# Gate products of a recurrence as pairs over 64 rows, with their activations in one table, in a hybrid decoder layer

## The chip, the cores and the metric

The kernel runs on one core of a Trainium2 chip. The metric is the device time of one execution in microseconds (us). Three runs of the kernel before took 961.67, 961.89 and 962.27 us; the median is 961.89 us.

A core has five engines that work at the same time, each on its own list of instructions in a fixed order: TensorE (PE, matrix products), VectorE (DVE), ScalarE (ACT, activation functions), GpSimd (POOL) and SyncE (SP, which here only issues DMAs). A product has two instructions on PE: a weight load (its row in the profile has the engine name PEld) and the matmul that streams the other operand through the array. Engines wait for each other through semaphores.

## The reference

One decoder layer over 1024 tokens and 16 meta tokens, model width 1024, feed-forward width 4096:

```
u = rmsnorm(h) ;  z = u @ w_in = [q | k | v | x_rec | y_rec]
B = sliding-window attention(q, k, v, sinks)                # 8 heads of 64
xr = causal depthwise conv of width 4 over x_rec            # 512 channels
gate_r = einsum("btnc,ncd->btnd", xr in 8 blocks of 64, w_a) + b_a
gate_i = einsum("btnc,ncd->btnd", xr in 8 blocks of 64, w_x) + b_x
r, i  = sigmoid(gate_r), sigmoid(gate_i)
log_a = -8 * r * softplus(-lambda) ;  a = exp(log_a)
u     = sqrt(-expm1(2 * log_a)) * (i * xr)
h_t   = a_t * h_(t-1) + u_t                                 # along the tokens
A = gelu(y_rec) * h
h += rmsnorm(concat(B, A) @ w_out)
h += rmsnorm(w_ff2 @ relu(w_ff1 @ rmsnorm(h))^2)
```

The gates are products with eight separate blocks of 64x64 weights, one for each 64 channels.

## The kernel before

Every product is made in three parts. An operand is split into a high part (fp32r, made by a cast) and a low part (what is left, made by a subtraction), and `mm3` (lines 122 to 128) multiplies high x high, high x low and low x high into one PSUM bank. The helper `split` (lines 93 to 100) makes the two parts: the cast on ACT (line 95) or on another engine (line 97), the subtraction on DVE (line 98).

The kernel runs in stages: norms, k, v and first q; attention over four head pairs, two halves each; gates and recurrence; output projection; the feed-forward part, in which most of the time is spent. The projections of further q, x_rec and y_rec columns are "fills": `next_fill` (lines 658 to 664) loads the weights of the fill after this one and issues the products of this one, and while attention waits for ACT or DVE, PE has these products. A scheduler of the framework sets the order of each engine's instructions from its own estimate of durations and from priorities. `deferred` (lines 73 to 76) lowers the priority of what is in it, `behind` (lines 105 to 113) fixes that one instruction stands after another in the schedule, without a semaphore, and `lut` (lines 81 to 91) keeps the activations that need a function table in the order in which the program writes them, since ACT holds one table at a time and a change of table is an instruction of its own (ACT_TABLE_LOAD).

The recurrence is held transposed: 512 channels as four chunks `c` of 128 channels (two blocks of 64) on the partitions, 1040 tokens along the free axis. Its steps are:

- The weights of the two gates are laid out as 128x128 matrices with two blocks of 64x64 on the diagonal and zeros elsewhere (`graw`, lines 683 to 693): POOL writes the zeros, four DMAs the blocks, and `split` makes `gh` and `gl`.
- `gates(c)` (lines 697 to 715): for each of two gates and each of three pieces of 348, 348 and 344 tokens, one `mm3` with all 128 rows, and one Sigmoid from PSUM, with the bias in it. That is 4 x 2 x 3 x 3 = 72 products. Then DVE multiplies the second gate by the conv output `xc[c]`.
- `decay(c)` (lines 719 to 723): Exp(-8 sp r) is `a`, and with t = Tanh(-4 sp r) the factor sqrt(1 - a^2) is sqrt(-t)(1 + a), which `recur` puts together; sp is the softplus of -lambda.
- `recur(c)` (lines 725 to 730): Sqrt on ACT, two products and the scan on DVE.
- `rec_out(c, half)` (lines 732 to 738): Gelu of the y projection, times the scan, and `split` into the operand of the output projection.

Sigmoid, Exp with Tanh, Sqrt and Gelu take different tables. The decays and the roots are done for chunks 0 and 1, then for 2 and 3. The output projection begins with 96 products whose operands come from attention (weight chunks 0 to 3) and goes on with those that need the recurrence (chunks 4 to 7). The weights `w_out` come in eight loads of 512 KB, `load_wo`; the buffers named `raw` (two of 512 KB) hold weights on their way to the split, and a load into one waits until the split of what it held is over. The split parts of `w_out` go to the tags `ws` and `a`. A name such as `ps_s` is a PSUM bank; `s`, `pt`, `o` and `acc` are two banks each.

## Time and profile before

| | |
|---|---|
| median of 3 runs | 961.89 us |
| the profiled execution | 959.9 us, span on the core 957.9 us |
| PE busy | 940.8 us (98%) |
| DVE busy | 669.9 us (70%) |
| ACT busy | 501.1 us (52%) |
| granted TensorE clock | 0.999 |
| gates: first gate product to the last | 199.4 to 218.1 us of the span |
| first product of the output projection | 230.8 us |

The span is the time from the first to the last instruction on the core; the profiled execution's own time is 2.0 us longer. A share of busy time is an average over stages: PE is the engine that is nearly always busy, and the question at each place is whether PE has something that it may do. Rows of the timeline give the start, the duration of one instruction (matmuls are pipelined, so a duration is longer than the distance to the next start), the engine, the line of the program and the tiles, and in brackets the idle time before it with what ended it.

### The profile page before, as it was taken

How to read it: one execution, taken by the hardware profiler on the slowest of the kernel's cores; microseconds unless marked ns; L12 is line 12 of the kernel's file. 1: busy time of each engine (PE TensorE's matmuls, PEld its weight loads, DVE VectorE, ACT ScalarE, POOL GpSimd, SP SyncE). 2: the span in 40 equal slices, each digit the busy share in tenths (PEclk: the TensorE clock that was granted, in tenths of full speed). 3: DMA queues.
4: the chain of work that ended last, by engine and by line, in shares of the span. 5: the costliest groups of instructions: out<-in, count | busy, mean ns of one | idle time of the engine just before them, and what ended most of it. 6: DMA issues, size and time to landing. Idle time of an engine off the chain costs nothing.

```text
span 957.9 us, 12381 instructions
## 1 busy us (share of the span) xinstructions
PE 940.8 (98%) x4654; PEld 789.2 (82%) x4654; DVE 669.9 (70%) x945; ACT 501.1 (52%) x822; POOL 157.0 (16%) x202
## 2 busy tenths in 40 slices
PE   7999999999999999999999999999999999999997
PEld 6999998888788877888888888888888888888886
DVE  5579989755955796575655556568557676779884
ACT  7556676469634563443555565654433343435441
POOL 4015656600021100000111001100111100003020
PEclk9999999999999999999999999999999999999999
DMA  8111101112235457675646466744677866567422
GB/s 289 51 49 41 38 9 45 38 62 67 87 133 176 141 181 236 190 260 188 212 154 219 155 195 188 234 156 122 161 181 191 199 219 195 178 193 159 112 87 88
DMA packets 85626, 140.74 MB, mean 147 GB/s; under 512 B 5784, under 2 KB 48936, under 8 KB 85568
## 3 DMA queue, kind: packets, MB, share of 16 engines
q1 hardware_dynamic: 75104, 108.51, 35.7%
q0 software_dynamic: 9600, 29.36, 11.9%
q10 hardware_dynamic: 864, 2.10, 0.6%
q8 instruction: 36, 0.59, 0.3%
q14 instruction: 22, 0.18, 0.1%
HBM read 115.70 MB, written 23.07 MB: 145 GB/s over the span
## 4 chain that ended last, share of the span: by engine, by line
PE 93%; ACT 3%; DVE 1%; issue 1%; DMA 0%; POOL 0%; DVEq 0%; SPq 0%; ACTq 0%
PE ps_acc L124 11%; PE ps_acc L125 11%; PE ps_acc L126 11%; PE ps_s L126 6%; PE ps_pt L124 6%; PE ps_s L125 6%; PE ps_s L124 6%; PE ps_pt L126 6%; PE ps_pt L125 6%; PE ps_o L124 5%; PE ps_o L126 5%; PE ps_o L125 5%; PE ps_o L585 1%; ACT c L82 1%; PE ps_o L836 1%
## 5 line engine op out<-in xcount | busy, mean ns | idle before, releaser
L95 ACT CAST ws<-raw 128x1024 fp32r<-128x1024 f32 (+1 forms) x70 | 71.8, 1026 | 120.5 <-PE ps_o L125 45.9
L98 DVE TENSOR_TENSOR ws<-raw,ws 128x1024 fp32r<-128x1024 f32 (+1 forms) x71 | 86.3, 1215 | 41.4 <-ACT ws L95 41.4
L124 PE MATMUL ps_acc<-a,ws 128*128 128x256 f32 (+2 forms) x256 | 85.2, 333 | 0.0
L125 PE MATMUL ps_acc<-a,ws 128*128 128x256 f32 (+2 forms) x256 | 84.9, 332 | 0.0
L126 PE MATMUL ps_acc<-a,ws 128*128 128x256 f32 (+2 forms) x256 | 84.8, 332 | 0.0
L98 DVE TENSOR_TENSOR b<-b,b 128x1024 fp32r<-128x1024 f32 (+2 forms) x48 | 57.6, 1201 | 29.3 <-PE ps_o L125 19.8
L95 ACT CAST ws<-e 128x1024 fp32r<-128x1024 f32 x42 | 43.9, 1045 | 58.2 <-PE ps_o L125 30.6
L95 ACT CAST b<-b 128x1024 fp32r<-128x1024 f32 (+2 forms) x48 | 49.4, 1030 | 35.0 <-DVE b L862 34.1
L98 DVE TENSOR_TENSOR ws<-e,ws 128x1024 fp32r<-128x1024 f32 x42 | 51.4, 1223 | 20.0 <-ACT ws L95 20.0
L575 POOL TENSOR_SCALAR_AFFINE_SELECT c<-c 128x512 fp32r<-128x512 f32 x64 | 55.7, 894 | 27.3 <-ACT c L95 15.3
L169 POOL TENSOR_TENSOR rs<-ms,half_pow 128x1 f32<-128x1 f32 (+1 forms) x29 | 21.3, 740 | 210.5 <-DVE ms L165 209.1
L126 PEld LDWEIGHTS ps_acc<-a,ws 128*128 128x128 f32 x256 | 48.2, 188 | 4.9
L124 PEld LDWEIGHTS ps_acc<-a,ws 128*128 128x128 f32 x256 | 48.2, 188 | 4.2
L125 PEld LDWEIGHTS ps_acc<-a,ws 128*128 128x128 f32 x256 | 48.2, 188 | 4.2
L124 PE MATMUL ps_acc<-ws,b 128*128 128x512 f32 (+1 forms) x120 | 46.3, 386 | 0.0
L125 PE MATMUL ps_acc<-ws,b 128*128 128x512 f32 (+1 forms) x120 | 46.1, 384 | 0.0
L126 PE MATMUL ps_acc<-ws,b 128*128 128x512 f32 (+1 forms) x120 | 46.0, 384 | 0.0
L125 PE MATMUL ps_pt<-ws,b 128*128 128x512 f32 x112 | 44.2, 395 | 0.6 <-DVE ws L98 0.6
L126 PE MATMUL ps_pt<-ws,b 128*128 128x512 f32 x112 | 43.9, 392 | 0.0
L124 PE MATMUL ps_pt<-ws,b 128*128 128x512 f32 x112 | 43.9, 394 | 0.0
L124 PE MATMUL ps_s<-ws,b 128*128 128x512 f32 x110 | 43.3, 395 | 0.0
L126 PE MATMUL ps_s<-ws,b 128*128 128x512 f32 x110 | 43.2, 393 | 0.0
(393 smaller groups left out, 2713.1 us busy)
## 6 DMA issues: line engine op xcount, KB each, us to landing
raw<-in_w_ff_dram SPq DMA_DIRECT2D x58, 512.0 KB, 4.3
e<-in_w_ff_dram SPq DMA_DIRECT2D x42, 512.0 KB, 4.1
raw<-in_w_in_dram SPq DMA_DIRECT2D x12, 512.0 KB, 3.9
d<-in_w_ff_dram SPq DMA_DIRECT2D x12, 512.0 KB, 3.8
s_dram<-d POOLq DMA_DIRECT2D x12, 512.0 KB, 3.9
e<-in_w_ff_dram POOLq DMA_DIRECT2D x10, 512.0 KB, 5.6
raw<-in_w_ff_dram POOLq DMA_DIRECT2D x10, 512.0 KB, 5.8
c<-in_x_dram SPq DMA_DIRECT2D x8, 512.0 KB, 8.1
```

Source lines behind the costliest of these rows:

```text
L82: ins = nc.scalar.activation(*args, **kwargs).ins
L95: nc.scalar.copy(hi, src)
L98: low = nc.vector.tensor_tensor(lo, src, f32(hi), op=ALU.subtract).ins
L124: nc.tensor.matmul(dst, lh, rh, start=start, stop=False, skip_group_check=True)
L125: nc.tensor.matmul(dst, lh, rl, start=False, stop=False, skip_group_check=True)
L126: last_mm[0] = nc.tensor.matmul(dst, ll, rh, start=False, stop=stop, skip_group_check=True).ins.name
L169: last_pow[0] = nc.gpsimd.tensor_tensor(rs[:n], ms[:n], half_pow[:n], op=ALU.pow).ins.name
L575: nc.gpsimd.affine_select(out=m[:, :, side, :], in_=f32(m)[:, :, 1, :], pattern=[[0, 4], [-sign, P]], compare_op=op, fill=0.0, base=0, cha ...
L585: nc.tensor.matmul(po[:, :, oc : oc + n], v, m[:, :, pc : pc + n], start=first and k == 0, stop=last and k == 1, skip_group_check=True,)
L836: nc.tensor.transpose(pt[:, i, :], xn[:, kc * P : (kc + 1) * P], ident)
```

## The change

The gates are computed otherwise, in six respects:

1. Gate products over 64 rows. The zeros are gone. One product takes one block of 64 rows (half of the array) against 128 columns: the 64 columns of `w_x` beside the 64 of `w_a`, in swapped order for the other half. So one product makes both gates of one block, and the two halves `s` of a chunk are two products on different rows into different PSUM banks, issued in turn. Their number stays at 72: 4 chunks x 3 pieces x 3 parts x 2 halves.
2. The two gates of a block then lie on different partitions. DVE moves the half that is in the wrong place: per chunk, two copies of 64x1040 and two instructions of 64x1040 for (1 + t) x in place of one of 128x1040.
3. Sigmoid is written as (1 + tanh(z/2))/2, with halved biases in a table `gbias` of four small DVE instructions. Tanh and Exp are in one table, so `decay` of a chunk stands right after the gates of the next chunk, and all four decays are done before the first Sqrt. All four Sqrt stand together, and the Gelus after them.
4. Held together by chunk: products of a chunk stand behind the last activation of the chunk before (`hold`), and most of the second piece of the fill of y chunk 1 stands behind the products of gate chunk 0 (`begun`).
5. The gate weights are loaded and cast in the middle of attention, through a `raw` buffer and without zeros; the split parts of the conv outputs (`gate_parts`) are made two chunks ahead.
6. Parts of the second weights chunk of `w_out` go to tag `e`, the broadcast of a norm weight and one early feed-forward operand to tag `a`, where they had been the other way about. The one small Sqrt that brings in the Sqrt table for the end of the kernel is put behind an instruction near the end; before, the scheduler had placed it at 246.9 us.

```diff
+            if (j, half) == (2, 1):
+                graw = slot("raw", [P, NLRU, 2, HD])
+                for s in range(2):
+                    r = HALF[s]
+                    for i, w in enumerate((w_x, w_a)):
+                        nc.sync.dma_start(
+                            graw[r, :, i ^ s, :], w[0, s::2].rearrange("n c d -> c n d")
+                        )
+                g_all = slot("b", [P, 2, NLRU, 2, HD], F32R)
+                gw = g_all[:, 0], g_all[:, 1]
+                with deferred(FILL_LAG):
+                    split(*gw, graw)
...
-    graw = slot("e", [P, 2, NLRU, P])
-    behind(last_pow[0], nc.gpsimd.memset(graw, 0.0).ins)
...
-    gh = slot("e", [P, 2, NLRU, P], F32R)
-    gl = slot("b", [P, 2, NLRU, P], F32R)
-    split(gh, gl, graw)
...
+    def gate_parts(c):
+        parts[c] = pair("b", [P, TT])
+        split(*parts[c], xc[c])
...
     def gates(c):
-        ch, cl = pair("b", [P, TT])
-        split(ch, cl, xc[c])
-        rg[c] = []
-        for i in range(2):
-            t_ = slot("c", [P, TT])
-            for t0, n in ((0, 348), (348, 348), (696, 344)):
-                flip[0] += 1
-                acc = bank(("s", "pt", "o")[flip[0] % 3])
-                mm3(
-                    acc[:, :n], (gh[:, i, c, :], gl[:, i, c, :]),
-                    (ch[:, t0 : t0 + n], cl[:, t0 : t0 + n]), True, True,
-                )
-                lut(
-                    t_[:, t0 : t0 + n], acc[:, :n], AF.Sigmoid,
-                    bias=prm[:, c, 5 + i : 6 + i],
-                )
-            rg[c].append(t_)
-        nc.vector.tensor_tensor(t_, t_, xc[c], op=ALU.mult)
+        halves_x = parts[c]
+        te, to = slot("b", [P, TT]), slot("c", [P, TT])
+        hold = shut[0]
+        for t0, n in ((0, 348), (348, 348), (696, 344)):
+            accs = []
+            for s in range(2):
+                flip[0] += 1
+                accs.append(bank(("s", "pt", "o")[flip[0] % 3]))
+            for k, (a, b) in enumerate(((0, 0), (0, 1), (1, 0))):
+                for s in range(2):
+                    ins = nc.tensor.matmul(
+                        accs[s][:, :n], gw[a][HALF[s], c], halves_x[b][HALF[s], t0 : t0 + n],
+                        start=k == 0, stop=k == 2, skip_group_check=True,
+                    ).ins
+                    if hold:
+                        behind(hold, ins)
+            if (c, t0) == (0, 696):
+                behind(ins.name, begun[1][1])
+            for s, t_ in enumerate((te, to)):
+                shut[0] = lut(
+                    t_[:, t0 : t0 + n], accs[s][:, :n], AF.Tanh, scale=0.5,
+                    bias=gbias[:, s, c : c + 1],
+                ).name
+        v = slot("c", [P, TT])
+        lo, hi = HALF
+        nc.vector.tensor_copy(v[hi], to[lo])
+        nc.vector.scalar_tensor_tensor(
+            to[lo], te[lo], 1.0, xc[c][lo], op0=ALU.add, op1=ALU.mult
+        )
+        nc.vector.tensor_copy(v[lo], te[hi])
+        nc.vector.scalar_tensor_tensor(
+            to[hi], to[hi], 1.0, xc[c][hi], op0=ALU.add, op1=ALU.mult
+        )
+        rg[c] = v, to, te
...
+    gate_parts(0)
+    gate_parts(1)
     for c in range(NLRU):
         gates(c)
+        if c + 2 < NLRU:
+            gate_parts(c + 2)
+        if c:
+            decay(c - 1)
+    decay(3)
     next_fill()
-    for cs in ((0, 1), (2, 3)):
-        for c in cs:
-            decay(c)
-        for c in cs:
-            recur(c)
+    for c in range(NLRU):
+        recur(c)
...
     split_wo(0, "ws", nc.vector)
-    for kc in range(1, 4):
+    split_wo(1, "e")
+    for kc in range(2, 4):
         split_wo(kc, "a")
...
-            lut(root, half_pow, AF.Sqrt, scale=-1.0)
+            behind(w_low[0], lut(root, half_pow, AF.Sqrt, scale=-1.0))
```

The scheduler works out a new order from this. On PE the gates of chunk 1 stood before between parts of the y fill as two gates by three pieces, each a run of three products over all rows (the names are the bank, then the split parts of the conv output and of the gate weights):

```order
L124 MATMUL ps_s_2569<-b_2564,e_2523 128x348
L125 MATMUL ps_s_2569<-b_2565,e_2523 128x348
L126 MATMUL ps_s_2569<-b_2564,b_2524 128x348
L124 MATMUL ps_pt_2574<-b_2564,e_2523 128x348
L125 MATMUL ps_pt_2574<-b_2565,e_2523 128x348
L126 MATMUL ps_pt_2574<-b_2564,b_2524 128x348
```

On PE now, the same place (after a product of the y fill, line 125 of the changed kernel; line 732 is the gate product; `ps_s` and `ps_pt`, then `ps_o` and `ps_s`, are the banks of the two halves):

```order
L125 MATMUL ps_acc_2338<-a_103,ws_2145 128x512
L732 MATMUL ps_s_2581<-b_2534,b_2033 128x348
L732 MATMUL ps_s_2581<-b_2535,b_2033 128x348
L732 MATMUL ps_s_2581<-b_2534,b_2033 128x348
L732 MATMUL ps_pt_2582<-b_2534,b_2033 128x348
L732 MATMUL ps_pt_2582<-b_2535,b_2033 128x348
L732 MATMUL ps_pt_2582<-b_2534,b_2033 128x348
L732 MATMUL ps_o_2591<-b_2534,b_2033 128x348
L732 MATMUL ps_s_2592<-b_2534,b_2033 128x348
L732 MATMUL ps_o_2591<-b_2535,b_2033 128x348
L732 MATMUL ps_s_2592<-b_2535,b_2033 128x348
```

In the second piece (`ps_o`, `ps_s`) the two halves stand in turn; in the first the scheduler has put three of one half and then three of the other. Nine of the twelve pieces stand in turn, three do not (here, one of chunk 2 and one of chunk 3, where two full products stand between the halves). The gate products now stand in six groups among products over all rows, so that PE goes over from all rows to halves and back twelve times.

On ACT, the end of the gates and what follows before (the names of line 82 are the result, then the operand and the scale):

```order
L82 ACTIVATE c_2642<-ps_o_2653,prm 128x344
L82 ACT_TABLE_LOAD
L82 ACTIVATE b_2728<-c_2531,m8sp 128x1040
L82 ACTIVATE c_2531<-c_2531,m4sp 128x1040
L82 ACTIVATE b_2731<-c_2568,m8sp 128x1040
L82 ACTIVATE c_2568<-c_2568,m4sp 128x1040
L82 ACT_TABLE_LOAD
L82 ACTIVATE c_2531<-c_2531 128x1040
L82 ACTIVATE c_2568<-c_2568 128x1040
L82 ACT_TABLE_LOAD
```

and now, from the last gate activation of chunk 3 to the Sqrts (the cast from `d_2775` is that of weights chunk 2 of `w_out`):

```order
L82 ACTIVATE c_2662<-ps_o_2684,gbias 128x344
L82 ACTIVATE b_2622<-c_2654,m4sp 128x1040
L82 ACTIVATE c_2654<-c_2654,m2sp 128x1040
L82 ACTIVATE b_2661<-c_2693,m4sp 128x1040
L96 CAST a_2787<-d_2775 128x1024
L82 ACTIVATE c_2693<-c_2693,m2sp 128x1040
L82 ACT_TABLE_LOAD
L82 ACTIVATE c_2570<-c_2570 128x1040
L82 ACTIVATE c_2611<-c_2611 128x1040
L82 ACTIVATE c_2654<-c_2654 128x1040
```

The table load ahead of the first Sqrt now stands behind all eight decay activations; before it stood behind four. On the whole list ACT has four table loads where it had eight.

On DVE, weights chunks 0 and 1 of `w_out` were split before after the first steps of the recurrence (line 728 is the first, line 97 the cast of chunk 0, `a_2769` the low part of chunk 1):

```order
L728 SCALAR_TENSOR_TENSOR c_2531<-b_2728,c_2531 128x1040
L97 CAST ws_2764<-raw_2756 128x1024
L640 COPY d_2413<-ps_acc_2440 128x512
L728 SCALAR_TENSOR_TENSOR c_2568<-b_2731,c_2568 128x1040
L729 TENSOR_TENSOR c_2547<-c_2547,c_2531 128x1040
L98 TENSOR_TENSOR ws_2765<-raw_2756,ws_2764 128x1024
L98 TENSOR_TENSOR a_2769<-raw_2758,a_2768 128x1024
```

and now before the half-height work of gate chunk 3, ahead of all recurrence steps:

```order
L98 CAST ws_2779<-raw_2771 128x1024
L647 COPY d_2421<-ps_acc_2448 128x512
L99 TENSOR_TENSOR e_2784<-raw_2773,e_2783 128x1024
L99 TENSOR_TENSOR ws_2780<-raw_2771,ws_2779 128x1024
L751 COPY c_2693<-b_2661 64x1040
L747 COPY c_2693<-c_2662 64x1040
L752 SCALAR_TENSOR_TENSOR c_2662<-c_2662,b_2023 64x1040
L748 SCALAR_TENSOR_TENSOR c_2662<-b_2661,b_2023 64x1040
L647 COPY d_2702<-ps_acc_2703 128x512
```

The two weight splits stand earlier, and four half-height instructions per chunk are added.

More of the change, by code (lines that the diff above doesn't have):

```diff
@@ L128, in mm3 @@
         ).ins.name
+        return ins
     last_mm = [None]
@@ L216, in norm_rows, with project @@
         return xn
-    def project(w, pieces, sink):
+    def project(w, pieces, sink, begun=None):
         wh, wl = w
@@ L228, in project @@
                 )
+                if kc == 1 and begun is not None:
+                    begun.append(ins)
             sink(acc[:, :n], t0, n)
@@ L680, in hybrid_layer @@
     attend(*prev)
[L683 to L693 removed]
+    gbias = const.tile([P, 2, NLRU], F32, name="gbias")
@@ L719, in decay @@
     def decay(c):
-        r = rg[c][0]
-        av[c] = slot("b", [P, TT])
-        lut(av[c], r, AF.Exp, scale=m8sp[:, c : c + 1])
-        lut(r, r, AF.Tanh, scale=m4sp[:, c : c + 1])
+        v, _, te = rg[c]
+        lut(te, v, AF.Exp, scale=m4sp[:, c : c + 1], bias=m4sp[:, c : c + 1])
+        lut(v, v, AF.Tanh, scale=m2sp[:, c : c + 1], bias=m2sp[:, c : c + 1])
     def recur(c):
-        r, gi = rg[c]
-        lut(r, r, AF.Sqrt, scale=-1.0)
-        nc.vector.scalar_tensor_tensor(r, av[c], 1.0, r, op0=ALU.add, op1=ALU.mult)
+        r, gi, a = rg[c]
@@ L729, in recur @@
+        lut(r, r, AF.Sqrt, scale=-0.25)
+        nc.vector.scalar_tensor_tensor(r, a, 1.0, r, op0=ALU.add, op1=ALU.mult)
         nc.vector.tensor_tensor(gi, gi, r, op=ALU.mult)
-        nc.vector.tensor_tensor_scan(r, av[c], gi, 0.0, op0=ALU.mult, op1=ALU.add)
+        nc.vector.tensor_tensor_scan(r, a, gi, 0.0, op0=ALU.mult, op1=ALU.add)
     def rec_out(c, half):
```

32 lines of the change are left out of this document (19 added, 13 removed).

## The prediction

> **What bounds the kernel now.** I read the page first: its span, the busy engines, the chain that ended last.
>
> ```profile
> span 957.9 us, 12381 instructions
> ...
> PE 940.8 (98%) x4654; PEld 789.2 (82%) x4654; DVE 669.9 (70%) x945; ACT 501.1 (52%) x822; POOL 157.0 (16%) x202
> ...
> PE 93%; ACT 3%; DVE 1%; issue 1%; DMA 0%; POOL 0%; DVEq 0%; SPq 0%; ACTq 0%
> ```
>
> PE is the bound over the whole: a product less is time saved, unless another engine is late at that place. So I looked at the stage from the first gate product to the end of DVE's recurrence, as a table of four stretches, with the limits where PE's kind of work changes.
>
> ```profile
> core 0: us, PE busy (x) PEld busy (x) DVE busy (x) ACT busy (x) POOL busy (x), PEclk, DMA share, GB/s
> 199.38:218.13 18.75, 18.75 (x105) 17.38 (x104) 6.03 (x6) 12.05 (x25) 0.00 (x0) 1.00 0.16 57
> 218.13:230.81 12.68, 12.68 (x57) 10.33 (x56) 5.52 (x7) 12.53 (x13) 0.00 (x0) 1.00 0.01 1
> 230.81:245.11 14.30, 13.16 (x57) 10.06 (x55) 14.30 (x14) 14.24 (x18) 0.00 (x0) 1.00 0.36 111
> 245.11:265.91 20.80, 20.80 (x90) 16.90 (x91) 20.80 (x23) 10.30 (x15) 0.00 (x0) 1.00 0.30 98
> ```
>
> In the gates (first row) PE has no gap and DVE is busy 6.03 of 18.75 us; from 230.81 us on DVE has no gap, and PE loses 14.30 - 13.16 = 1.14 us. These are the two waits, from PE's timeline, and the instructions that end them, from DVE's and ACT's:
>
> ```profile
> 231.98 0.63 PE L124 MATMUL ps_s<-ws,b 128*128 128x512 f32 x2
> 233.16 0.50 PE L125 MATMUL ps_pt<-ws,b 128*128 128x512 f32 x1 [0.56 <-DVE ws L98]
> 231.89 1.22 DVE L98 TENSOR_TENSOR ws<-raw,ws 128x1024 fp32r<-128x1024 f32 x1
> 245.11 0.50 PE L124 MATMUL ps_pt<-a,b 128*128 128x512 f32 x1 [0.58 <-ACT a L95]
> 244.03 1.03 ACT L95 CAST a<-raw 128x1024 fp32r<-128x1024 f32 x1
> ```
>
> Both wait for split weights of `w_out`. So the stage has three candidates: PE's products, the splits of `w_out`, and the recurrence on DVE, which PE needs some 24 us after the output projection begins.
>
> **The change, part by part.** *Gate products.* Their price, from PE's timeline (first, and the last three with what follows):
>
> ```profile
> 199.38 0.32 PE L124 MATMUL ps_s<-b,e 128*128 128x348 f32 x1
> ...
> 217.66 0.32 PE L124 MATMUL ps_o<-b,e 128*128 128x344 f32 x1
> 217.82 0.32 PE L125 MATMUL ps_o<-b,e 128*128 128x344 f32 x1
> 217.98 0.32 PE L126 MATMUL ps_o<-b,b 128*128 128x344 f32 x1
> 218.13 0.39 PE L124 MATMUL ps_acc<-a,ws 128*128 128x512 f32 x1
> ```
>
> Start to start a gate product takes 0.16 us, and 72 of them 72 x 0.159 = 11.4 us. The change keeps the number and the streamed columns; all that it can save is that two products on different halves run at once. In the order nine pieces have three pairs each (27 pairs), and three pieces have two runs of three. A pair costs at least 0.159 us (full overlap) and at most 0.318 (none). Between the ends stands the weight load: two loads per pair. Two rows of this trace bound its pace, products over all rows with 128 columns, and products over 8 rows with 8 columns:
>
> ```profile
> 60.84 0.27 PE L529 MATMUL ps_s<-km,b 128*128 128x128 f32 x1
> 60.95 0.28 PE L525 MATMUL ps_s<-b,b 128*128 128x128 f32 x1
> ...
> 53.27 0.32 PEld L439 LDWEIGHTS ps_o<-ident,d 8*128 8x128 f32 x4 [0.17 <-issue]
> ```
>
> The first follow each other in 0.11 us, though 128 columns should stream in a quarter of the time of 512 (0.24 us: the pair at 231.98 takes 0.63, one of them 0.39), so 0.11 us is the pace of a full-height load, and two one after the other make 0.22. The second, each 0.133 to 0.138 us long and four in 0.32 us, follow in 0.062 us: two in 0.124, below 0.159. The half-height load is nearest to the second, as the only one in the trace that takes a part of the rows, so I take 0.17 for a pair. The runs of three overlap in one place at most: 5 + 5 + 6 = 16 slots of 0.159. Sum 27 x 0.17 + 16 x 0.159 = 7.1 us, a saving of 4.3 us (4.6 at best, 0 at worst).
>
> *Going over from all rows to a part and back.* PE's rows around the four 8-row products show what this costs:
>
> ```profile
> 52.96 0.38 PE L286 MATMUL ps_s<-ident,d 128*128 128x128 f32 x2
> 53.27 0.41 PE L439 MATMUL ps_o<-ident,d 8*128 8x8 f32 x4
> 53.61 0.44 PE L497 MATMUL ps_pt<-ident,c 128*128 128x128 f32 x2
> ```
>
> The second L286 product started at 52.96 + 0.11 = 53.07; the next was due at 53.18 and came at 53.27, with the idle weight load of 0.17 us above. On the way back the next was due 0.062 after 53.48, at 53.54, came at 53.61, and the one after it 0.06 later than usual. That is 0.09 + 0.13 = 0.22 us for both ways, 0.11 to 0.12 for one. Twelve of them cost 1.4 us. Nothing is the lower end, 0.35 us each the upper (the last product's overlap of 0.32 - 0.16 and a weight load of 0.19 laid bare), 4.2 us in all.
>
> *Splits of `w_out`.* On DVE they now stand ahead of the recurrence, on ACT among the decays. Chunk 1's load is held back: its `raw` buffer is free when the last y weights are split, which the order puts after gates of chunk 1. I lay it out by ACT's rows:
>
> ```profile
> L82 ACT ACT_TABLE_LOAD  x7: 1283/1283/1283, 198.3 to 245.6; - x7
> L82 ACT ACTIVATE c<-ps_s,prm x8: 550/552/562, 200.8 to 217.4; 128x348 f32<-128x348 f32 x8
> L82 ACT ACTIVATE b<-c,m8sp x4: 1147/1159/1168, 220.2 to 232.5; 128x1040 f32<-128x1040 f32 x4
> L82 ACT ACTIVATE c<-c,m4sp x4: 1161/1165/1167, 221.4 to 234.5; 128x1040 f32<-128x1040 f32 x4
> L82 ACT ACTIVATE c<-c x4: 1057/1067/1075, 226.1 to 238.0; 128x1040 f32<-128x1040 f32 x4
> ...
> 206.12 0.55 ACT L82 ACTIVATE c<-ps_s,prm 128x348 f32<-128x348 f32 x1 [1.58 <-PE ps_s L126]
> 206.60 0.55 ACT L82 ACTIVATE c<-ps_pt,prm 128x348 f32<-128x348 f32 x1
> ```
>
> From the first gate activation to the first Sqrt ACT has now 24 activations of 0.55 (0.48 apart), eight decays of 1.16, five casts of 1.03 (0.95 apart) and one table: 11.5 + 9.3 + 4.8 + 1.3 = 27 us. It also waits: about 2 us between chunks 0 and 1, where PE has 19 full products (4.4 us) while ACT has 3 us of work, and about 2 us for chunk 1 of `w_out`. So the first Sqrt comes near 199 + 31 = 230 us, after 226.1 before, but with all decays behind it. Chunks 0 and 1 of `w_out` are split by then 10 us earlier than before, chunk 3 before the Gelus and not among them: both PE waits go, -1.1 us (0 to -1.14). The four table loads saved (5.1 us of ACT) are worth nothing by themselves: PE waits for none of them.
>
> *DVE.* Rows for the half-height work and the recurrence:
>
> ```profile
> 177.52 1.67 DVE L613 SCALAR_TENSOR_TENSOR b<-d,prm,b 128x1039 f32<-128x1039 f32 x1
> ...
> 218.91 1.24 DVE L715 TENSOR_TENSOR c<-c,b 128x1040 f32<-128x1040 f32 x1 [3.69 <-ACT c L82]
> 227.23 1.24 DVE L728 SCALAR_TENSOR_TENSOR c<-b,c 128x1040 f32<-128x1040 f32 x1 [4.75 <-ACT c L82]
> 228.39 0.69 DVE L97 CAST ws<-raw 128x1024 fp32r<-128x1024 f32 x1
> ...
> 264.01 1.91 DVE L98 TENSOR_TENSOR b<-d,b 128x512 fp32r<-128x512 f32 x3
> ```
>
> A duration goes by the length of a row, so half the partitions save nothing: four instructions per chunk cost 2 x 0.6 + 2 x 1.15 = 3.5 us where one cost 1.15, 9.4 us more in all. It lies in the first two stretches, where DVE was idle 12.72 + 7.16 us. A copy may also cost 1.24, as two-operand work does; I take 0.69, the one-operand row. From its first step to its last subtraction DVE had 38.7 us without a gap (227.23 to 265.92). Less is left in this tail now: two subtractions of the `ws` and `a` splits, one more of chunk 2, a cast and two copies stand ahead, 3 x 1.14 + 0.6 + 2 x 0.6 = 5.2 us. The tail begins near 231.5 and ends near 231.5 + 33.5 = 265, about 1 us earlier than before, while PE is 4 us earlier. PE's order asks for the first low part of the recurrence 12 products (2.8 us) later than before, so most of this fits; I count a new wait of 0.8 us behind these parts (0 to 2.5).
>
> *The rest.* What the change adds outside the stage, by these rows (ACT's busy tenths in 40 slices of 24 us, and one short DVE instruction at the place of the four new ones):
>
> ```profile
> ACT  7556676469634563443555565654433343435441
> ...
> L468 DVE TENSOR_SCALAR sm<-sm x1: 170/170/170, 55.6 to 55.6; 128x4 f32<-128x4 f32 x1
> ```
>
> The gate weights' cast and subtraction cover 512 instead of 1024 columns and move into attention, where ACT and DVE wait in turn; four small loads pass SP's queue ahead of three y loads, and POOL writes no zeros. The Sqrt table of 1.28 us moves to where ACT is busy some 4 tenths of the time. I cost all this at nothing; four DVE instructions of 0.17 us that found no gap would cost 0.7 us, a late table load up to 1.3.
>
> Sum: -4.3 + 1.4 - 1.1 + 0.8 = -3.2 us. On the profiled execution's 959.9 that is 956.7; the median of the runs is 961.89, 2.0 above it, and gives 958.7.
>
> **The rivals.** *Weight loads take turns.* If two half-height loads go at the full-height pace, a pair costs 0.22 us; 27 x 0.22 + 2.5 = 8.4, a saving of 3.0, and with 1.4, -1.1 and a smaller wait of 0.3 the time falls by 2.4 to 959.5. For it speaks the 0.11 row, against it the 0.062 row. The Trainium skill, "TensorE: Matmul & The Clock Gate", section "LDWEIGHTS (loading the stationary operand)", says that a load's time goes by its columns and not by its rows, 128 columns in about 107 ns; that would be this rival, and the 8-row loads, also of 128 columns, do not agree with it.
>
> *No overlap.* The pairs run one after the other, the change doesn't do what it says: 0 + 1.4 - 1.1 + 0 = +0.3, 962.2. No product of the trace shows two at once, so nothing excludes it.
>
> *The recurrence's tail becomes the bound* (the other side). Place: the first low part that PE waits for behind DVE. Price: each microsecond by which the tail ends later than 265 goes to the time. It decides from 5.1 us on, 3.2 to win back and 1.9 for a measurable loss. If the eight copies cost 1.24 and the other eight 1.67 as in the L613 row, it is 8 x 0.55 + 8 x 0.43 = 7.8 us later at most, less what falls into DVE's gaps; with 6 us the time is 964.7. Against it: DVE's 20 us of gaps in the first two stretches.
>
> **How the numbers follow.** A difference under 0.2% (1.9 us) I take for no change. Forecast 0.5, weight loads in turn 0.18, no overlap 0.17, late tail 0.10, something better than the sum (cheaper switches, no new wait: 956 to 957) 0.05. Faster: 0.5 x 0.88 + 0.18 x 0.8 + 0.05 = 0.63; slower: 0.10 and 0.03 of no overlap with dear switches, 0.13; same 0.24. The range: 4.6 saved, switches at nearly nothing and both waits gone give 961.9 - 5.2 = 956.7 at the low end; at the high end no overlap with 0.17 per switch, 962.8. Outside it are left the late tail and dear switches.
>
> **What would show it.** Gate products of a pair that start within some 0.02 us of each other, pairs 0.17 apart; an idle weight load near 0.1 us at each of twelve changes; no wait for a split of `w_out` between 226 and 245; DVE's last subtraction of the recurrence near 262 to 265 on the span, and a PE wait behind it. Wrong it would be if the pairs follow in 0.3 us, or if PE waits for the recurrence by over 2.5 us.

## The result, and the profile after

The changed kernel takes 959.09 us (median of 12 runs, 957.82 to 960.75), the kernel before 961.96 us beside it (12 runs). The ratio is 0.9975, with a 95% interval of 0.9967 to 0.9983. In a second comparison, on another occasion, the same kernel took 959.37 us against 960.58: a ratio of 0.9989 (0.9979 to 0.9998). Both intervals lie below 1, so the changed kernel is faster; by how much is known only to a microsecond or two (2.9 us on the first occasion, 1.2 on the second, which the prediction's own limit of 0.2% would call no change). Runs of either kernel scatter by 2 to 4 us, in part for a reason that the section on the hardware shows, so the accounts below go by one stage of the traces: from the start of the 1201st product on PE (175.6 us in the kernel before, in the last part of attention) to that of the 1641st (271.8 us there, in the output projection). Nearly all that the change touches lies between, and all kernels here have the same 4654 products.

The profiled execution took 959.18 us, its span is 957.5. First the busy time, and the stretches that answer to those shown of before (from the first gate product to the last, to 231, the waits, the recurrence's tail; columns as there):

```profile
PE 938.8 (98%) x4654; PEld 783.6 (82%) x4654; DVE 680.5 (71%) x961; ACT 494.9 (52%) x818; POOL 156.4 (16%) x201
```

```profile
core 0: us, PE busy (x) PEld busy (x) DVE busy (x) ACT busy (x) POOL busy (x), PEclk, DMA share, GB/s
198.36:218.90 20.54, 20.54 (x126) 15.69 (x125) 16.26 (x17) 16.16 (x26) 0.00 (x0) 1.00 0.08 27
218.90:231.00 12.10, 12.10 (x54) 9.83 (x53) 9.44 (x12) 9.20 (x13) 0.00 (x0) 1.00 0.40 132
231.00:245.00 14.00, 14.00 (x63) 11.34 (x62) 12.29 (x11) 13.55 (x17) 0.00 (x0) 1.00 0.22 75
245.00:266.00 21.00, 20.13 (x86) 15.76 (x85) 21.00 (x23) 6.54 (x10) 0.00 (x0) 1.00 0.24 79
```

In the third row PE has lost its two waits for `w_out` (14.00 of 14.00), in the fourth it has new ones (20.13 of 21.00). DVE, busy 6.03 of 18.75 us of the gates before, is busy 16.26 of 20.54 now. Next PE's timeline at the gates of chunk 1: the last full-height product, the first four pairs, the last pair, and the way back.

```profile
204.23 0.40 PE L125 MATMUL ps_acc<-a,ws 128*128 128x512 f32 x1
204.56 0.43 PE L732 MATMUL ps_s<-b,b 64*128 64x348 f32 x1
204.57 0.42 PE L732 MATMUL ps_pt<-b,b 64*128 64x348 f32 x1
204.82 0.32 PE L732 MATMUL ps_s<-b,b 64*128 64x348 f32 x1
204.83 0.32 PE L732 MATMUL ps_pt<-b,b 64*128 64x348 f32 x1
204.98 0.32 PE L732 MATMUL ps_s<-b,b 64*128 64x348 f32 x1
205.00 0.32 PE L732 MATMUL ps_pt<-b,b 64*128 64x348 f32 x1
205.14 0.31 PE L732 MATMUL ps_o<-b,b 64*128 64x348 f32 x1
205.15 0.32 PE L732 MATMUL ps_s<-b,b 64*128 64x348 f32 x1
...
205.93 0.32 PE L732 MATMUL ps_pt<-b,b 64*128 64x344 f32 x1
205.95 0.32 PE L732 MATMUL ps_o<-b,b 64*128 64x344 f32 x1
206.20 0.50 PE L128 MATMUL ps_acc<-a,ws 128*128 128x512 f32 x1
```

Two products start 0.01 to 0.02 us apart and the next two 0.16 us later: the pairs run at once. The switch is dear: after 204.23 a product was due at 204.46 and came at 204.56, the second pair came 0.26 and not 0.16 later, and the same happens on the way back. Last the waits that are new in the stage, from PE's timeline:

```profile
186.20 0.97 PE L591 MATMUL ps_o<-c,b 128*128 128x512 f32 x5 [0.29 <-POOL c L581]
...
193.59 0.47 PE L125 MATMUL ps_acc<-a,ws 128*128 128x512 f32 x1 [0.19 <-DVE b L647]
...
255.73 0.51 PE L129 MATMUL ps_pt<-a,b 128*128 128x512 f32 x1 [0.42 <-DVE b L99]
...
262.02 0.50 PE L129 MATMUL ps_pt<-a,b 128*128 128x512 f32 x1 [0.46 <-DVE b L99]
```

A wait costs more than its bracket: the bracket begins only where the profile ends the product before, 0.39 to 0.40 us after its start, while the next product would have started after 0.23. Counted in starts that come later than the usual distance, the four cost 0.55, 0.43, 0.68 and 0.72 us (each with the product behind it, which is 0.1 late), and the two that are gone had cost 0.83 and 0.85.

The stage, added up from the starts of its 440 products:

| | before | after | difference |
|---|---|---|---|
| 72 gate products, by slots of 0.159 us | 11.4 | 39 slots, 6.2 | -5.2 |
| 12 switches, 0.21 us each | 0 | 2.5 | +2.5 |
| two waits for splits of `w_out` | 1.7 | 0 | -1.7 |
| waits at 186 and 194 us | 0 | 1.0 | +1.0 |
| waits behind the recurrence's tail | 0 | 1.4 | +1.4 |
| stage, 1201st to 1641st product | 96.26 | 94.17 | -2.1 |

The rows add up to -2.0; the rest is rounding. From there the gain stays between 2.1 and 2.4 us for 480 us, and about one of it is given back at 762.7 us, where PE waits 0.97 us for split feed-forward weights whose transfer is late. The second execution of the changed kernel has that wait too (0.77), the profiled one of before doesn't; what brings it was not looked into. Some more is lost in small pieces, and at the last product 0.7 us of the gain is left, 1.0 in the second execution.

### The profile page after: what moved, and what is told of

It reads as the page before. It is cut to its first block, busy times and chain, and to the rows that moved or that the text cites. A ratio compares the mean times of both kernels' runs of the same rounds, so it can differ in the third digit from the quotient of the medians.

```text
span 957.5 us, 12397 instructions
## 1 busy us (share of the span) xinstructions
PE 938.8 (98%) x4654; PEld 783.6 (82%) x4654; DVE 680.5 (71%) x961; ACT 494.9 (52%) x818; POOL 156.4 (16%) x201
## 4 chain that ended last, share of the span: by engine, by line
PE 89%; DVE 6%; issue 2%; ACT 1%; DMA 1%; POOL 1%; DVEq 0%; SPq 0%; ACTq 0%; POOLq 0%
PE ps_acc L125 10%; PE ps_acc L128 10%; PE ps_acc L129 10%; PE ps_pt L129 6%; PE ps_pt L125 6%; PE ps_pt L128 6%; PE ps_s L129 6%; PE ps_s L128 6%; PE ps_s L125 6%; PE ps_o L129 5%; PE ps_o L128 5%; PE ps_o L125 5%; PE ps_o L591 1%; DVE c L767 1%; PE ps_o L878 1%
```

## The experiments

Each kernel's stage time stands beside its total; the stage of the changed kernel was 94.17 and 94.07 us in two executions, so smaller differences than 0.2 us are not read; two executions are a thin measure for that. The medians are good to 1 to 2 us only: that of the kernel before was 960.58 to 961.96 us on five occasions. Each ratio is to the kernel before on the same occasion. Line numbers are each kernel's own.

**The same kernel again.**

> The changed kernel itself once more, as the measure for the other kernels on this chip: 959.1 within the scatter of its runs (957.8 to 960.8), and in its profile the same waits as before: 0.45 us at the second group of attention products near 186, 0.35 us near 193.6, and 0.57 and 0.61 us behind the recurrence's low parts. If the waits move between executions of one kernel, they are scatter and not its order.

Measured: 959.37 us, stage 94.07. The waits are those of the first execution, without the products behind them 0.31, 0.35, 0.59 and 0.64 us by starts where that had 0.45, 0.35, 0.57 and 0.61. They belong to the order, not to the execution.

**The pairs on the same rows.**

```diff
-                        accs[s][:, :n], gw[a][HALF[s], c], halves_x[b][HALF[s], t0 : t0 + n],
+                        accs[s][:, :n], gw[a][HALF[0], c], halves_x[b][HALF[0], t0 : t0 + n],
```

> The changed kernel, but both products of a pair take the weights and the data of the first 64 rows. The gates of the second half are then made from the wrong operands, so the output is another; the number, size and order of all instructions stay. Theory 'halves at once' (two products run together because they stand on different halves): every pair now takes 2 x 0.159 us, so the gate products take 72 slots instead of 39, +33 x 0.159 = +5.2 us at the end of the gates. The two waits behind the recurrence's tail (0.57 and 0.61 us) go, since PE comes later: about +4 us in all, 963. Rival 'nothing runs at once that matters' (the gain came from the order of the splits and the table alone): within 1 us of the changed kernel, 959. A second reading, that half-height products are paced by their weight loads and not by their columns, would show a spacing other than 0.159 us.

Measured: 963.07 us, ratio to before 1.0020 (1.0009 to 1.0031), stage 97.96. Chunk 1's first piece, from PE's timeline:

```profile
205.47 0.74 PE L732 MATMUL ps_s<-b,b 64*128 64x348 f32 x3
206.06 0.64 PE L732 MATMUL ps_pt<-b,b 64*128 64x348 f32 x3
206.54 0.32 PE L732 MATMUL ps_o<-b,b 64*128 64x348 f32 x1
```

The three products of one half now run ahead of the three of the other; the second three take 0.48 us. When the gates are done the kernel is 5.18 us later than the changed one, 33 x 0.159 = 5.2; its switches cost 0.21 us each as well; the two waits at the tail are gone, 5.18 - 1.40 = 3.8 in the stage. So overlap on different rows is what the pairs bring. This is also the kernel of the rival "no overlap", and it is slower than before, by 1.7 us in the stage.

**All rows again, the rest of the change kept.**

```diff
+                graw = slot("raw", [P, 2, NLRU, P])
+                nc.gpsimd.memset(graw, 0.0)
...
+        for i in range(2):
+            t_ = slot("c", [P, TT])
+            for t0, n in ((0, 348), (348, 348), (696, 344)):
...
+                for k, (a, b) in enumerate(((gh, ch), (gh, cl), (gl, ch))):
+                    ins = nc.tensor.matmul(
+                        acc[:, :n], a[:, i, c, :], b[:, t0 : t0 + n],
...
+                shut[0] = lut(
+                    t_[:, t0 : t0 + n], acc[:, :n], AF.Tanh, scale=0.5,
+                    bias=gbias[:, c, i : i + 1],
+                ).name
+        nc.vector.scalar_tensor_tensor(
+            t_, t_, 1.0, xc[c], op0=ALU.add, op1=ALU.mult
+        )
```

> One part undone: gate products over all 128 rows with the zeros again, 72 of them one after the other, no half-height copies on DVE; the one table with Tanh, the order by chunk, all decays ahead of the Sqrts, the early cast and the other tiles for w_out stay. Theory 'pairs pay, the order pays through the two w_out waits': against the changed kernel the products cost 33 x 0.159 = 5.2 us more and the switches about 12 x 0.2 = 2.5 us less, +2.7; the recurrence's tail begins some 3 us earlier (no half-height work ahead of it) and PE is later, so its two waits go, -1.2: +1.5 us, 960.5, still 1.3 below the kernel before. Rival 'the order and the table bring all of it': 959 or less. Rival 'the pairs bring all of it': 962, as the kernel before.

Measured: 962.69 us, ratio 1.0010 (1.0000 to 1.0019), stage 96.37: no gain against before, where 1.3 us were expected. The two waits for `w_out` are gone here too, and nothing waits at the tail. What took them back is the end of attention, in the list of PE's waits (sum, times, longest):

```profile
PE ps_o L591 <- POOL c L581: 1.0, 1, 1.0
```

By starts this one costs 1.3 us and the one near 195 us 0.43: 1.7 lost, 1.7 won. But the changed kernel loses only 0.55 us at the first of these places, and this kernel differs from it there too: with the zeros the gate weights are twice as wide, and their subtraction on DVE, some 10 us before the wait, takes 1.21 us in place of 0.68 (this kernel, then the changed one):

```profile
177.19 1.21 DVE L99 TENSOR_TENSOR b<-raw,b 128x1024 fp32r<-128x1024 f32 x1
```

```profile
175.94 0.68 DVE L99 TENSOR_TENSOR b<-raw,b 128x512 fp32r<-128x512 f32 x1
```

So this kernel gains nothing in the stage without the pairs, but up to 0.75 us of what it loses may be the price of the zeros and not of the rest of the change; the two were not parted. The median is 1.3 us above before; the stage explains 0.1 of it, and the profiled execution was already 1.5 us late at 34 us, before anything that was edited.

**Pairs, with Sigmoid and eight table loads.**

```diff
-                    t_[:, t0 : t0 + n], accs[s][:, :n], AF.Tanh, scale=0.5,
+                    t_[:, t0 : t0 + n], accs[s][:, :n], AF.Sigmoid,
...
-        if c:
-            decay(c - 1)
-    decay(3)
     next_fill()
-    for c in range(NLRU):
-        recur(c)
+    for cs in ((0, 1), (2, 3)):
+        for c in cs:
+            decay(c)
+        for c in cs:
+            recur(c)
```

> The other part undone: pairs as in the changed kernel, but Sigmoid with its own table, and the decays and roots in two groups (chunks 0 and 1, then 2 and 3) as before, so ACT loads its tables eight times again. PE's order is that of the changed kernel. Theory 'table loads are worth nothing by themselves': PE waits for none of them in the gates; 959 to 960, and the first recurrence steps start earlier than 233 us. Rival 'the one table pays': the 5 us of ACT come back in part as PE waits between 199 and 270 us, 961 or more.

Measured: 960.38 us, ratio 0.9994 (0.9982 to 1.0005), stage 94.23, the same as with one table. There are two waits between 199 and 270 us, one for a `w_out` cast and one for a high part of the recurrence:

```profile
234.50 0.73 PE L125 MATMUL ps_pt<-a,b 128*128 128x512 f32 x2 [0.18 <-ACT a L96]
...
258.33 0.72 PE L125 MATMUL ps_pt<-a,b 128*128 128x512 f32 x2 [0.66 <-ACT b L96]
```

By starts they cost 1.37 us, where the two waits at the changed kernel's tail cost 1.40. So by the stage the one table is worth nothing, as the theory said, but as a net of two pairs of waits at different places; that a table load costs nothing by itself isn't shown by this. The median, 1.3 us above the changed kernel's, would say otherwise. The profiled execution had 1.5 us of slow clock at 158 us, before the gates, which is of that size, but for the other runs this is not shown.

**Gates in four groups, always in turn.**

```diff
+        chain = [None]
...
-                for s in range(2):
+                for s in (1, 0) if c else (0, 1):
...
+                    if chain[0]:
+                        behind(chain[0], ins)
+                    if c:
+                        chain[0] = ins.name
```

> The changed kernel with the products of each gate chunk chained in one order, always in turn, with no full-height product between: four groups instead of six, 36 pairs instead of 33 pairs and 6 single products. Theory 'pairs at 0.159 and 0.2 us a switch': the last gate product comes (3 x 0.159) + (4 x 0.2) = 1.3 us earlier. Behind it two theories part: if the recurrence's tail on DVE sets the time, PE waits for it longer by what it comes earlier, and the time stays at 959; if the tail has room, the time falls to 957.8.

Measured: 958.23 us, ratio 0.9973 (0.9963 to 0.9983), stage 93.28. The gates with their switches take 1.3 us less, as the slots and 0.21 us a switch say. In place of two waits there is one longer one,

```profile
PE ps_pt L129 <- DVE b L99: 1.5, 1, 1.5
```

which costs 1.74 us by starts where the two had cost 1.40. So the tail took back 0.34 of the 1.3, and the stage kept 0.9. Neither theory has it whole: the new order of PE also moved steps on DVE, and the tail began at 232.0 and not at 233.3.

**Gate weights split after attention.** The block with `graw`, its four DMAs and its split stands behind the loop over attention again, with no lowered priority.

> One part of the change undone: the gate weights are loaded and split after attention, as before, and not in its middle; everything else stays. PE's order then has 12 products of the y fill again between the two last groups of attention products, where the changed kernel has none. Theory 'the early cast costs a wait at the end of attention': the wait of 0.45 us at 186 (with the late product behind it 0.55) goes, and what follows comes 0.55 us earlier; 958.5 if the recurrence's tail follows, 959.1 if the tail takes it back. Rival 'the early cast was needed': the first gate product waits for the weights, 0.5 us or more later than 198.4.

Measured: 959.26 us, ratio 0.9991 (0.9982 to 1.0000), stage 94.18. The wait at 186 us is gone and the first gate product isn't late (it comes 0.2 us earlier, counted from the 1201st product). But the gain of 0.55 us is given back at three places: the wait near 193 grows from 0.35 to 0.65 us, the first at the tail from 0.57 to 0.80, the second from 0.61 to 0.65.

**Both edits.** The chain and the late gate weights together.

> Both edits together: gate products chained in four groups, always in turn, and the gate weights split after attention. If the two add up: 958.2 - 0.55 = 957.7. If the tail of the recurrence on DVE is the bound by now, it is as the chained kernel alone, 958.2, and the wait at the first low part grows from 1.64 towards 2.2 us.

Measured: 958.23 us, ratio 0.9976 (0.9965 to 0.9986), stage 93.00: 0.3 us below the chained kernel, the 0.55 of the early wait less 0.30 at 193 us. The wait at the tail is 1.67 us, as with the chain alone: the tail moves along with the gates.

**Four subtractions on GpSimd.**

```diff
+        if kc < 4:
+            split(wo[kc][0], wo[kc][1], wo_raw[kc], eng)
+        else:
+            hi, lo = wo[kc]
+            nc.scalar.copy(hi, wo_raw[kc])
+            nc.gpsimd.tensor_tensor(lo, wo_raw[kc], f32(hi), op=ALU.subtract)
```

> As the kernel with both edits, and the four subtractions for weights chunks 4 to 7 of w_out on GpSimd, which is idle there, instead of DVE. DVE has four steps of 1.14 us less in the recurrence's tail. Theory 'the tail is a queue on DVE': the waits for the low parts (1.64 us and what follows) go, PE runs on without a gap from 245 to 270, and the time falls by 1.2 to 1.7 us against that kernel: 956.0 to 956.5. Rival 'the tail waits for ACT or for the scans and not for the weight splits': the wait stays and the time too. Second rival: GpSimd takes over 2.5 us for each and slows DVE's steps, and PE waits for the low part of a w_out chunk instead.

Measured: 967.7 us, ratio 1.0069 (1.0056 to 1.0082), stage 102.55. The second rival held in its first half, far beyond its size: GpSimd took 5.34, 3.40, 3.33 and 2.79 us for its four steps, and DVE's steps beside them were slowed. But PE then waited for the first low part of the recurrence, on DVE, and not for one of `w_out`. The first two steps on GpSimd, a step on DVE beside the first of them, and PE behind:

```profile
241.61 5.34 POOL L797 TENSOR_TENSOR a<-d,a 128x1024 fp32r<-128x1024 f32 x1 [55.13 <-ACT a L796]
246.91 3.40 POOL L797 TENSOR_TENSOR a<-raw,a 128x1024 fp32r<-128x1024 f32 x1
```

```profile
244.66 3.39 DVE L770 TENSOR_TENSOR c<-c,c 128x1040 f32<-128x1040 f32 x1
```

```profile
262.04 0.79 PE L129 MATMUL ps_pt<-a,b 128*128 128x512 f32 x1 [7.21 <-DVE b L99]
```

The DVE step takes 1.24 us elsewhere, 3.39 here. PE waits 7.21 us for the first low part. The theory was not tested by this, since the edit slowed the queue that it was to shorten.

**The rule on the y fill taken out.**

```diff
-            if (c, t0) == (0, 696):
-                behind(ins.name, begun[1][1])
```

> The kernel with the chained gates and the late gate weights, and the rule taken out that puts most of the second piece of y chunk 1 behind the gates of chunk 0 (the part of the change called 'held together' for the fill). The fill then has 24 products on each PSUM bank before the next, where the rule leaves 3 on one. Theory 'the wait at 193 us is the rule's: the third bank is asked for 0.7 us after the first is full, before DVE has copied it': the wait of 0.65 us there goes, with the late product behind it 0.73, and the recurrence's tail moves along with the gates, so that the time falls by 0.7 to 957.5. Rival: the tail is held by something else (the w_out transfers), the wait for the low part grows from 1.67 to 2.4 us, and the time stays at 958.2.

Measured: 961.96 us, ratio 1.0004 (0.9992 to 1.0017), stage 96.97. The wait at 193 us did go, and with it 0.73 us. (The gates of chunk 0 still start 0.2 us later, since four more products of the fill now stand ahead of them.) But the scheduler's new order on DVE has a cast, a copy and a subtraction between the half-height steps of chunk 3, and ACT waits for the last of these (its row in ACT's timeline):

```profile
230.27 1.26 ACT L82 ACTIVATE b<-c,m4sp 128x1040 f32<-128x1040 f32 x1 [1.93 <-DVE c L750]
```

So the tail begins later, counted from the last gates, and PE waits 3.36 us for the first low part. Then comes a second price, in the table of stretches:

```profile
252.00:258.80 6.80, 3.44 (x15) 2.44 (x14) 6.80 (x7) 2.51 (x3) 0.00 (x0) 0.90 0.30 122
258.80:264.30 5.50, 5.50 (x13) 4.34 (x14) 5.50 (x8) 3.02 (x6) 0.00 (x0) 0.51 0.32 98
264.30:270.00 5.70, 5.70 (x26) 4.61 (x26) 3.34 (x6) 0.38 (x1) 0.00 (x0) 1.00 0.60 184
```

After the wait PE has a granted clock of 0.51 for 5.5 us: 13 products in the time of 24, 2.6 us more. The rival had the place, but not the size.

**The scans behind the first low part.** On the kernel just shown (`scans` keeps the scan instructions as they are made):

```diff
+            behind(low.name, scans[2], scans[3])
```

> The same kernel, and on DVE the scans of chunks 2 and 3 put behind the low part of chunk 0's first half; no instruction more or less. If the wait at the first low part is one of order on DVE (the scans of two later chunks and the multiplication stand ahead of it), the 1.67 us there shrink to 0 to 0.4 us, now at the high part of chunk 2, and the time is 1.3 to 1.7 us below the kernel beside it, 955.8 to 956.2. If DVE's tail is simply too long, the wait moves whole to a later part of chunks 1 to 3, and the time stays.

Measured: 955.60 us, ratio 0.9939 (0.9927 to 0.9951), stage 91.23. No wait at a low part is left, and with it went the slow clock. In this kernel it was the order on DVE: the low part that PE asks for first stood behind two scans that nobody waits for at that time.

**The same edit alone on the changed kernel.**

> The changed kernel, and only the scans of chunks 2 and 3 on DVE put behind the low part of chunk 0's first half. DVE's steps laid end to end from the first recurrence step at 233.3 give that low part at 253.4 (PE asks for it near 254.0) and that of chunk 1 at 259.6 (PE asks near 258.2). Theory 'the tail begins too late, by the wait of ACT for chunk 3's half-height work': the first wait goes, and one of about 1.4 us comes at chunk 1's low part, so the time stays at 959.1. Rival 'order alone is the cause': both waits go and the time is 957.7.

Measured: 959.24 us, ratio 0.9978 (0.9968 to 0.9988), stage 94.79, 0.6 us more than the changed kernel's. As the rows gave it, the wait moves to chunk 1's low part, 1.33 us by starts, with 0.43 at a high part before it. Order alone isn't enough where the tail begins at 233.2.

**Chain, late weights and tail order, with the rule on the y fill.**

> The fastest kernel so far with one rule put back, the one that holds most of y chunk 1's second piece behind the gates of chunk 0. Its DVE order does chunk 3's half-height work ahead of the w_out splits, so the tail begins at 232 and not at 234 us. By the rows: the wait at 193 us comes back (0.65 and 0.08), no wait at the low parts: 0.7 above 955.6, 956.3. Rival: the wait at 193 is swallowed by what comes after, and the time is 955.6 as well; then the rule did no harm once the tail is in order.

Measured: 955.53 us, ratio 0.9943 (0.9930 to 0.9956), stage 91.22, the same as without the rule. This kernel is the one of "both edits" with the order of the scans alone added, so it is the cleanest measure of that order: 93.00 to 91.22 us, and the wait of 1.67 us, 1.78 with the product behind it, is gone. The wait at 193 is there again (0.65 us by starts). The kernel without the rule loses as much at two high parts of the recurrence (0.24 and 0.20 us, each with 0.11 behind it); its tail begins later, at 233.9 and not at 232.0. DVE's timeline shows the order that PE needs:

```profile
249.16 1.28 DVE L780 TENSOR_TENSOR b<-b,c 128x512 f32<-128x512 f32 x2
250.36 0.68 DVE L99 TENSOR_TENSOR b<-d,b 128x512 fp32r<-128x512 f32 x1
250.96 4.53 DVE L772 TENSOR_TENSOR_SCAN c<-b,c 128x1040 f32<-128x1040 f32 x2
255.41 1.20 DVE L99 TENSOR_TENSOR a<-d,a 128x1024 fp32r<-128x1024 f32 x1
256.53 0.68 DVE L99 TENSOR_TENSOR b<-b,b 128x512 fp32r<-128x512 f32 x1
```

The first low part is done at 250.96, in the changed kernel at 255.6. These two kernels beat both, by 5.8 to 5.9 us against before, and are some 3.5 us below the changed kernel's medians.

## Why the prediction was right, and where its terms were not

The forecast of 958.7 us and the measured 959.09 agree, and the range held. The main step was right: products on different halves run at once. That the totals agree to 0.4 us is in part luck. The sum of -3.2 us was -2.1 by the stage, -0.7 at the last product of the two profiled executions, and -1.2 by the medians of the second occasion. The single terms are further off, and their errors partly cancel.

- *Gate products, -4.3 predicted, -5.2 measured.* The pairs cost 0.159 us and not 0.17, the lower bound. And the step "the runs of three overlap in one place at most" failed: in the rows above, three products of `ps_s` and three of `ps_pt`, which PE's list has as three and then three, ran as pairs. Only chunk 3's piece, with two full-height products between its halves, ran singly: 33 pairs and 6 single products.
- *Switches, +1.4 predicted, +2.5 measured.* The place and the number were right; the price of 0.12 us, taken from products over 8 rows, is 0.21 here. The error is of the other sign and nearly as large, so that the two terms together, -2.9 predicted and -2.7 measured, look better than either.
- *Splits of `w_out`, -1.1 predicted, -1.7 measured.* Both waits went. The term was mis-sized since it counted the idle time of the brackets, and a wait also sets back the start of its product and of the next. They are gone without the pairs too, and without the one table but for one of 0.34 us, so neither of the two is needed for most of it; which part does it was not tried alone.
- *DVE's tail, +0.8 predicted, +1.4 measured.* The copies cost 0.70 us as taken, and the tail was 33.5 us long to a tenth. But the forecast had it begin at 231.5, and it began at 233.3, so it ended at 266.8 and not at 265. The layout of ACT's rows left out one wait. ACT's and DVE's timelines of the changed kernel show it:

```profile
226.66 1.26 ACT L82 ACTIVATE b<-c,m4sp 128x1040 f32<-128x1040 f32 x1 [2.09 <-DVE c L748]
...
230.90 1.28 ACT L82 ACT_TABLE_LOAD   x1
232.20 3.00 ACT L82 ACTIVATE c<-c 128x1040 f32<-128x1040 f32 x3
```

```profile
222.66 0.70 DVE L751 COPY c<-b 64x1040 f32<-64x1040 f32 x1
...
225.39 1.23 DVE L748 SCALAR_TENSOR_TENSOR c<-b,b 64x1040 f32<-64x1040 f32 x1
...
233.30 2.39 DVE L765 SCALAR_TENSOR_TENSOR c<-b,c 128x1040 f32<-128x1040 f32 x2 [1.72 <-ACT c L82]
```

  The last decay overwrites a tile that the last half-height step still reads, so four DVE steps stand between the last gate activation and the last decay, and all four Sqrt behind them.
- *"The rest" at nothing, +1.0 measured.* This is the step that failed outright; the rule on the y fill has no term in the sum at all. The early cast changed PE's order near 186 us: the two last groups of attention products stand back to back, where before 12 products of the y fill stood between, and the second waits for GpSimd. The rule on the y fill leaves three products on one PSUM bank before a third bank is asked for, before DVE has copied it. Each was taken away in an experiment, and each time its own wait went.
- *Table loads worth nothing.* As a net it held in the stage: eight loads and four give 94.23 and 94.17 us.

Of the rivals, weight loads in turn is refuted: two half-height loads fit into 0.159 us. The loads of a pair start together, from the rows of the weight loads at the first two pairs of chunk 1:

```profile
204.56 0.18 PEld L732 LDWEIGHTS ps_s<-b,b 64*128 64x128 f32 x1 [0.36 <-issue]
204.57 0.18 PEld L732 LDWEIGHTS ps_pt<-b,b 64*128 64x128 f32 x1
204.67 0.19 PEld L732 LDWEIGHTS ps_s<-b,b 64*128 64x128 f32 x1
204.68 0.19 PEld L732 LDWEIGHTS ps_pt<-b,b 64*128 64x128 f32 x1
```

The Trainium skill, "TensorE: Matmul & The Clock Gate", section "LDWEIGHTS (loading the stationary operand)", gives 107 ns for 128 columns by its formula; two such loads one behind the other would make 0.214 us a pair, as an estimate. The trace shows that loads on different halves don't stand one behind the other. No overlap is the kernel with the same rows: it was put at 962.2, 0.3 us above before, and took 963.07. In the stage it is 1.7 above: the switches cost 1.1 us more than forecast and the waits at 186 and 193 us 1.0, and the splits of `w_out` brought 0.6 more. The late tail came as a wait of 1.4 us and not as the bound.

## What to carry over

A term of a sum is only as good as the nearest row: a price from products over 8 rows was off by three quarters for products over 64. When work moves on one engine, the scheduler's order moves on all of them, and the small waits that come of it (1.0 and 1.4 us here) are together as large as the gain; look in the new order for what stands ahead of the first thing the bounding engine will ask for. Here a subtraction of 0.68 us that may pass two scans brought 1.8 us in the stage, on top of gates in contiguous groups and late gate weights; on the changed kernel alone it brought nothing. The three edits together took the stage from 94.17 to 91.22 us, more than the 2.1 us of the change itself.

## What the runs showed of the hardware

*Products on different halves pass each other.* Three and three in the list ran in pairs, 0.01 us apart (204.56 and 204.57 above), also in chunk 2. With both halves on the same rows, the same list ran three and three (205.47 and 206.06 above). The Trainium skill, "TensorE: Matmul & The Clock Gate", section "Part 3: Packing small matmuls — row/col tiling", says that products start and end strictly in the order of the program. The starts here don't agree.

*A wait can cost twice.* After waits of 3.36 and 7.21 us the clock was 0.51 and 0.54 for over 5 us, 12 or 13 products at 0.43 us in place of 0.23; after one of 1.5 us in the chained kernel it stayed at 1.00. The same page of the Trainium skill, "TensorE: Matmul & The Clock Gate", Part 1, says that the clock falls to half after an idle window of about 3.4 us. Here less was enough: the clock fell within the two waits, at 257.4 and 257.2 us, 1.9 and 2.4 us after the last product before had ended. And in attention, where every profiled execution waits about 0.43 and 1.26 us within 2 us of each other, it falls in four of the 14 profiled executions only. The same Part 1 of the Trainium skill says that the hardware's window runs freely, so that it would matter where a wait falls in it; no run here can show that. The same kernel, twice, as a table of stretches (the execution with the fall, then the one without):

```profile
158.40:162.00 3.60, 3.60 (x20) 3.60 (x19) 3.47 (x13) 2.27 (x9) 1.22 (x1) 0.53 0.02 5
```

```profile
158.40:162.00 3.60, 3.53 (x30) 3.56 (x31) 3.50 (x12) 2.59 (x11) 0.37 (x2) 1.00 0.10 28
```

It costs 1.5 us in each of the four profiled executions that have it (23.3 us in place of 21.8 for the same 156 products). This is one source of the scatter of the runs, in a place that no edit here touches.

*DVE's two-operand steps stand beside GpSimd's.* The DVE step at 244.66 took 3.39 us in place of 1.24 beside a GpSimd subtraction; it ended at 248.05, 1.1 us after that subtraction (246.95). Three later multiplications of 0.68 us took 2.8 to 2.9 us, and each ended 0.55 us after a GpSimd step. So it looks as if each had stood until GpSimd's step was done; a scan beside the first GpSimd step took its usual 2.32 us. The GpSimd steps took 2.79 to 5.34 us; how long one takes with no DVE work beside it, no run shows. The Trainium skill, "GPSIMD Engine Reference", section "1. Specifications", says that the two share their SBUF interfaces, with contention when a DVE instruction has two SBUF inputs. The trace agrees for the multiplications, and not for the scan, which reads two tiles as well.
